# Reordered split, modulation and gate work in a hybrid decoder layer, with the last FFN block kept on the core

## The chip, the core and the metric

The kernel runs on one core of a Trainium2 chip. A core has TensorE (PE, matmuls into PSUM), VectorE (DVE), ScalarE (ACT), GpSimd (POOL) and SyncE (SP), which here issues the DMA transfers; each engine takes its own instructions in its own order and waits on semaphores for the others. The metric is the device time of one execution in microseconds (us), the median over runs.

## The reference

One decoder layer on a sequence of 1024 tokens with 1024 channels, all in float32:

```python
mod = silu(c) @ w_ada + b_ada                      # adaLN: six vectors of 1024
shift1, scale1, gate1, shift2, scale2, gate2 = split(mod, 6)
h = rmsnorm(x, norm1_w) * (1 + scale1) + shift1
qa, ka, va, iq, ik, iw, qr, kr, vr, gr, ga, gb = split(h @ w_in)      # 7240 columns
# attention: 8 heads of 64; a light indexer scores all keys, each query keeps its 256 best
y_a = sparse_attention(rope(qa), rope(ka), va, top256(indexer(iq, ik, iw))) @ w_attn_proj
# retention: 4 heads, keys of 128, values of 256, chunks of 128 tokens with a decayed state
y_r = (silu(gr) * head_groupnorm(retention(rot(qr), rot(kr), vr), gn_w)) @ w_ret_proj
x = x + gate1 * ((sigmoid(ga) * y_a + sigmoid(gb) * y_r) @ w_out)
h2 = rmsnorm(x, norm2_w) * (1 + scale2) + shift2
x = x + gate2 * ((silu(h2 @ w_ffn_gate) * (h2 @ w_ffn_up)) @ w_ffn_down)   # 2816 wide
return rmsnorm(x, final_norm_w)
```

## The kernel before

**Precision.** Each float32 matmul is done as three matmuls of rounded parts. A factor is split into a high part (a copy to a rounded type, ScalarE) and a low part (source minus high part, VectorE or GpSimd), and the product is high x high + high x low + low x high. A split is thus two instructions on two engines. In the names of tiles the endings `hi` and `lo` are these parts. `split_weight` (L70) splits projection weights, `split_block` (L760) the factors of the blocked products.

**Seven products instead of eight.** The gate, q and k projections, the FFN's two up products and the down product are multiplied by a Strassen-Winograd scheme: a 2 x 2 split of both factors, seven products `M1` to `M7` of block sums. Per stream of 256 weight columns (`class Stream`, L765) `ORDER` is M1, M5, M6, M3, M7, M2, M4; the token side's sums lie split in the tiles h11, S1, S2, S4, S3, h21, h22 (`SIDE`, L755). M1, M6, M7 and M4 accumulate in one PSUM bank, which is copied after M1 and M6 and added after M7; M5 and M3 share another. One product is 12 matmuls of 128 x 512. `run` (L873) emits the products of a sequence in order, prepares (loads, sums, splits) each factor two or three products ahead, and calls `behind(i)` after each product to place other work.

**Stages in order.** adaLN for the first norm; normed input `hT`; indexer; V of the attention with the indexer scores; retention, two heads at a time (`hp` = 0, 1), first Q and K for eight token tiles (rotation on GpSimd, transposes on TensorE), then V with the chunk work (`inner`, `chunk`); the gate streams (`flow`: four for gr, two for qa, two for ka, one for gb, four for ga); the retention projection; attention; merge; output projection with the second norm (`put_half1`, `put_half2`, `put_rest` split the normed tiles into the sides `h11`, `S1`, `h22`, `h21`); the FFN's 22 streams (`FfnEnv`), whose activations (`act_d`) and weight sums (`dw_d`) go through memory; the down product, which reads them back (`draw`) and splits them (`dslot`); final norm.

**Side work on VectorE.** The rest of adaLN (`mod_work`, L508) is a generator of 36 steps: four vectors of eight products of a 128 x 1024 weight tile (`mw`, two buffers, 512 KB a load on SP's queue) and one step that finishes the vector. Before, 16 steps lie beside the attention's V, 8 beside Q, K of heads 0 and 1, 9 beside their V, the rest after it. The selection of the 256 best (`select_all`, L449) is 32 counting passes of six instructions, a strict chain on VectorE. It has a low priority and fills holes; `passes` holds each pass's first instruction, and `turns_after(a, b)` only orders a after b on their engine, without a semaphore.

**What sets the order.** The kernel's text gives priorities, and a scheduler that simulates the engines' times lays out each engine's order from them; the orders given by `turns_after` bind it. So an edit at one place can move instructions elsewhere.

**Rotary part of q and k.** The qa and ka streams store their first 16 rows a head to `rot_d` and the rest to `q_d`, `k_d`. `rope_load` reads `rot_d` back, `rope_store` rotates it, splits it and stores it to `q_d` and `k_d` with eight DMAs a call.

## Time and profile before

| | |
|---|---|
| median of 3 runs | 1771.59 us (1771.57 to 1774.38) |
| the profiled execution | 1770.31 us, its span 1768.4 us |
| TensorE | busy 1696.3 us, 8266 matmuls, mean granted clock 0.991 |
| VectorE | busy 1216.7 us, 2099 instructions |
| ScalarE | busy 757.2 us, 1469 instructions |
| GpSimd | busy 882.4 us, 873 instructions |
| DMA | 266.48 MB, mean 151 GB/s |

"Busy" is the time in which an engine executes. A row of the waits names the engine, its line and tile, and what it waited for. A timeline row gives the start, the duration, the engine, the kernel's line, the operation with output and inputs, and in brackets the idle time before it and what ended it. PEld is TensorE's load of weights, which overlaps its matmuls.

### The profile page before, as it was taken

How to read it: one execution, taken by the hardware profiler on the slowest of the kernel's cores; microseconds unless marked ns; L12 is line 12 of the kernel's file. 1: busy time of each engine (PE TensorE's matmuls, PEld its weight loads, DVE VectorE, ACT ScalarE, POOL GpSimd, SP SyncE). 2: the span in 40 equal slices, each digit the busy share in tenths (PEclk: the TensorE clock that was granted, in tenths of full speed). 3: DMA queues.
4: the chain of work that ended last, by engine and by line, in shares of the span. 5: the costliest groups of instructions: out<-in, count | busy, mean ns of one | idle time of the engine just before them, and what ended most of it. 6: DMA issues, size and time to landing. Idle time of an engine off the chain costs nothing. (4 is left out here: it accounts for less than half of the span.)

```text
span 1768.4 us, 24625 instructions
## 1 busy us (share of the span) xinstructions
PE 1696.3 (96%) x8266; PEld 1393.6 (79%) x8266; DVE 1216.7 (69%) x2099; ACT 757.2 (43%) x1469; POOL 882.4 (50%) x873
## 2 busy tenths in 40 slices
PE   5899989999999999999999999899999999999998
PEld 4797768888878887788777888688787778787887
DVE  7529793888998687574675747865756565686665
ACT  3625533333544444430676146533333333444444
POOL 3563275683544678430355631054544445556564
PEclk9999999999999999999999999999999999999999
DMA  9535452512333355964843720134444444597762
GB/s 276 161 99 169 149 162 62 149 39 57 117 90 131 112 172 176 291 182 146 196 116 136 244 98 1 54 107 165 158 156 160 137 150 143 203 320 247 209 183 107
DMA packets 182654, 266.48 MB, mean 151 GB/s; under 512 B 13872, under 2 KB 111616, under 8 KB 180096
## 3 DMA queue, kind: packets, MB, share of 16 engines
q1 hardware_dynamic: 182528, 264.91, 48.1%
q8 instruction: 65, 1.06, 0.3%
q14 instruction: 61, 0.50, 0.1%
HBM read 195.39 MB, written 69.47 MB: 150 GB/s over the span
## 5 line engine op out<-in xcount | busy, mean ns | idle before, releaser
L80 POOL TENSOR_TENSOR wlo<-wraw,whi 128x512 fp32r<-128x512 f32 (+2 forms) x116 | 147.0, 1279 | 105.3 <-ACT whi L77 86.3
L463 DVE TENSOR_SCALAR_CACHE_REDUCE eq<-score,cand 128x384 uint8<-128x384 f32 (+2 forms) x192 | 180.5, 940 | 3.6
L762 POOL TENSOR_TENSOR flo<-tmp,fhi 128x512 fp32r<-128x512 f32 x79 | 107.1, 1356 | 139.7 <-ACT fhi L761 111.8
L121 PE MATMUL mm<-whi,hT_hi 128*128 128x512 f32 (+1 forms) x432 | 159.8, 376 | 3.8 <-ACT qk L650 1.8
L124 PE MATMUL mm<-whi,hT_lo 128*128 128x512 f32 (+1 forms) x432 | 161.5, 376 | 0.0
L123 PE MATMUL mm<-wlo,hT_hi 128*128 128x512 f32 (+1 forms) x432 | 160.3, 374 | 0.0
L838 PE MATMUL ya<-hc,fhi 128*128 128x512 f32 x344 | 134.6, 392 | 2.3 <-DVE c L821 1.4
L1604 DVE TENSOR_TENSOR dslot<-draw,dslot 128x512 fp32r<-128x512 f32 x88 | 94.7, 1107 | 58.4 <-ACT dslot L1603 54.2
L1603 ACT ACTIVATE dslot<-draw 128x512 fp32r<-128x512 f32 x154 | 90.4, 626 | 102.9 <-DMA draw<-dw_d 23.4
L840 PE MATMUL ya<-hc,fhi 128*128 128x512 f32 x344 | 133.9, 389 | 0.0
L842 PE MATMUL ya<-hc,flo 128*128 128x512 f32 x344 | 132.4, 389 | 0.0
L1604 POOL TENSOR_TENSOR dslot<-draw,dslot 128x512 fp32r<-128x512 f32 x66 | 98.0, 1498 | 65.4 <-ACT dslot L1603 61.7
L762 POOL TENSOR_TENSOR flo<-raws,fhi 128x512 fp32r<-128x512 f32 x60 | 82.1, 1369 | 92.7 <-ACT fhi L761 64.2
L77 ACT ACTIVATE whi<-wraw 128x512 fp32r<-128x512 f32 (+2 forms) x116 | 67.0, 590 | 112.0 <-DMA wraw<-in_w_in_dram 46.4
L840 PE MATMUL yb<-hc,fhi 128*128 128x512 f32 x256 | 100.6, 393 | 6.1 <-DVE hc L1295 6.1
L842 PE MATMUL yb<-hc,flo 128*128 128x512 f32 x256 | 100.7, 394 | 3.2 <-POOL flo L762 3.2
L761 ACT ACTIVATE fhi<-tmp 128x512 fp32r<-128x512 f32 x84 | 53.0, 631 | 113.1 <-PE ya L840 61.4
L838 PE MATMUL yb<-hc,fhi 128*128 128x512 f32 x256 | 100.6, 394 | 0.6 <-DVE c L821 0.4
L121 PEld LDWEIGHTS mm<-whi,hT_hi 128*128 128x128 f32 x432 | 80.9, 188 | 16.0 <-ACT qk L650 2.2
L1144 POOL TENSOR_SCALAR sx<-sx,mx 128x128 f32<-128x128 f32 (+7 forms) x64 | 47.8, 752 | 88.0 <-DVE mx L1143 65.1
L124 PEld LDWEIGHTS mm<-whi,hT_lo 128*128 128x128 f32 x432 | 81.3, 189 | 12.7 <-issue 0.5
L807 DVE TENSOR_TENSOR tmp<-raws 128x512 f32<-128x512 f32 x40 | 39.5, 989 | 74.3 <-POOL flo L762 74.3
(410 smaller groups left out, 4950.9 us busy)
## 6 DMA issues: line engine op xcount, KB each, us to landing
draw<-act_d SPq DMA_DIRECT2D x77, 256.0 KB
mw<-in_w_ada_dram SPq DMA_DIRECT2D x32, 512.0 KB
act_d<-c SPq DMA_DIRECT2D x64, 256.0 KB
raw<-in_w_in_dram SPq DMA_DIRECT2D x26, 512.0 KB
raws<-in_w_ffn_gate_dram SPq DMA_DIRECT2D x24, 512.0 KB
raws<-in_w_ffn_up_dram SPq DMA_DIRECT2D x24, 512.0 KB
dw<-in_w_ffn_down_dram SPq DMA_DIRECT2D x22, 512.0 KB
dw_d<-dw SPq DMA_DIRECT2D x11, 1024.0 KB
```

The lines of the kernel that those rows point to most:

```text
L77: ins = nc.scalar.activation(hi[:, :n], raw[:, :n], AF.Copy)
L80: nc.gpsimd.tensor_sub(lo[:, :n], raw[:, :n], f32(hi[:, :n]))
L121: ins = nc.tensor.matmul(ps, lhsT=ahi, rhs=whi[:, :n], start=(i == 0), stop=False)
L123: nc.tensor.matmul(ps, lhsT=ahi, rhs=wlo[:, :n], start=False, stop=False)
L124: nc.tensor.matmul(ps, lhsT=alo, rhs=whi[:, :n], start=False, stop=(i == last))
L463: ins = [nc.vector.tensor_scalar(eq[:, :sc.shape[1]], sc, thr[j], None, op0=op, op1=ALU.add, accum_out=cnt[:, j:j + 1]) for j, sc in enume ...
L762: (eng or nc.gpsimd).tensor_sub(lo, src, f32(hi))
L838: mm = nc.tensor.matmul(ps, lhsT=whi[:, k, :], rhs=hhi[:, k, :], start=own and k == 0, stop=False, skip_group_check=True)
L840: nc.tensor.matmul(ps, lhsT=whi[:, k, :], rhs=hlo[:, k, :], start=False, stop=False, skip_group_check=True)
L842: nc.tensor.matmul(ps, lhsT=wlo[:, k, :], rhs=hhi[:, k, :], start=False, stop=k == 3, skip_group_check=True)
L1603: nc.scalar.activation(slot[:, 0], raw, AF.Copy)
L1604: lo_eng.tensor_sub(slot[:, 1], raw, f32(slot[:, 0]))
```

## The change

- **adaLN:** no step of `mod_work` lies beside Q, K of heads 0 and 1 any more; two steps a tile, instead of one, lie beside their V. The passes get other places to stay behind: numbers 7 to 10 in V of heads 0, 1 and 18 to 21 in V of heads 2, 3 (before 1 to 3 in Q, K, 4 to 7 and 16 to 19), and from number 24 every seven products in the gate streams (before from 22 every six).
- **Gate streams:** the first two run M1, M5, M6, M2, M3, M7, M4; their low parts stay on VectorE five products longer; the last two streams' low parts go to VectorE instead of GpSimd. Both `rope_load` calls come at the stream of gb and both `rope_store` calls at the first ga stream; before, the second of each came one stream later.
- **Start of the FFN:** the last normed tile's `h11` and `h21` splits, the first factors and S2 come in a fixed order ahead of the later sums and splits (`in_turn`); the first two streams compute t1 early and in place; M6 stands ahead of M4; S4 and S3 are split three products later.
- **FFN streams:** M4 of a stream comes behind M1 of the next.
- **Last block of the FFN (p = 10):** its activations and weight sums aren't stored and loaded again; the down product splits them where they lie. The final norm's weights lie in two tiles instead of one, the squares in one scratch tile.

```diff
-    mod_ins = [None]
...
                 turns_after(ins, behind)
-            mod_ins[0] = ins
             yield
...
             nc.scalar.activation(qkT[t // 2][:, t % 2].rearrange("p h t -> p (h t)"), tp, AF.Copy)
-            if hp == 0:
-                next(mgen, None)
-                if t in (2, 4, 6):
-                    turns_after(passes[t // 2], mod_ins[0])
         slots = [rows_slot([(w_in, C_VR + 2 * DV * hp, 2 * DV)], k) for k in range(KT)]
...
             if t and t % 2 == 0:
-                turns_after(passes[(3, 15)[hp] + t // 2], chunked[0])
+                turns_after(passes[(6, 17)[hp] + t // 2], chunked[0])
             if hp == 0:
-                next(mgen, None)
+                for _ in range(2):
+                    next(mgen, None)
             elif t == 2:
...
         ins = nc.scalar.activation(hi, src, AF.Copy)
-        (eng or nc.gpsimd).tensor_sub(lo, src, f32(hi))
-        return ins
+        return ins, (eng or nc.gpsimd).tensor_sub(lo, src, f32(hi))
...
             self.early = ()
-            self.next = None
+            self.next = self.t1 = None
...
+        def sum_early(self):
+            b = self.blocks
+            self.t1 = b["12"]
+            nc.vector.tensor_sub(self.t1, b["12"], b["11"])
...
             elif m == "M4":
-                src = self.t2
-                nc.vector.tensor_sub(src, b["21"], src)
+                src = b["21"] if m in self.early else self.t2
+                self.env.in_turn(None, nc.vector.tensor_sub(src, b["21"], self.t2))
+            elif m == "M7" and "M4" in self.early:
+                src = four(self.env.tmp())
+                self.env.in_turn(None, nc.vector.tensor_sub(src, self.t2, b["11"]))
             else:
                 x, y = {"M5": ("12", "11"), "M6": ("22", None), "M7": ("22", "12")}[m]
-                if m == "M6" and "M5" in self.early:
+                if m == "M6" and "M5" in self.early and not self.t1:
                     self.t1 = src
-                    nc.vector.tensor_sub(src, b["12"], b["11"])
-                nc.vector.tensor_sub(src, b[x], b[y] if y else self.t1)
+                    self.env.in_turn(None, nc.vector.tensor_sub(src, b["12"], b["11"]))
+                self.env.in_turn(None, nc.vector.tensor_sub(src, b[x], b[y] if y else self.t1))
                 if m == "M5":
             hi, lo = self.env.slot()
-            self.split = split_block(src, hi, lo, self.env.lo_engine)
+            self.split, self.lo = split_block(src, hi, lo, self.env.lo_engine)
+            self.env.in_turn(self.split, self.lo)
             return hi, lo
...
+        def in_turn(self, *_):
+            pass
...
...
-    seq = [(st, m) for m in ORDER for st in flow[:2]]
+    seq = [(st, m) for m in ("M1", "M5", "M6", "M2", "M3", "M7", "M4") for st in flow[:2]]
     seq += [(st, m) for st in flow[2:-2] for m in ORDER]
...
         n, m = 2 + (i - 14) // 7, seq[i][1]
-        if i == 6:
-            genv.lo_engine = None
-        if i >= 15 and (i - 15) % 6 == 0 and 22 + (i - 15) // 6 < len(passes) - 1:
-            turns_after(passes[22 + (i - 15) // 6], genv.added)
+        if i in (11, n_mid - 4):
+            genv.lo_engine = None if i == 11 else nc.vector
+        if i >= 15 and (i - 15) % 7 == 0 and 24 + (i - 15) // 7 < len(passes) - 1:
+            turns_after(passes[24 + (i - 15) // 7], genv.added)
         if 14 <= i < n_mid:
                 flow[n].next = flow[n + 1]
-            if n in (8, 9) and m == "M1":
-                rope[n - 8] = rope_load(n - 8)
-            if n in (9, 10) and m == "M5":
-                rope_store(n - 9, *rope[n - 9])
+            if n == 8 and m in ("M1", "M7"):
+                rope[len(rope)] = rope_load(len(rope))
+            if n == 9 and m in ("M5", "M2"):
+                rope_store(int(m == "M2"), *rope[int(m == "M2")])
         if i == n_mid:
...
         hi, lo = (c[:, :, o:o + P] for c in combo[name])
-        nc.scalar.activation(hi, src, AF.Copy)
-        nc.vector.tensor_sub(lo, src, f32(hi))
+        ins = nc.scalar.activation(hi, src, AF.Copy)
+        return ins, nc.vector.tensor_sub(lo, src, f32(hi))
...
         h11, h21, h12, s1 = parts_of(o)
-        put_combo("h11", o, h11)
-        nc.vector.tensor_sub(s1, s1, h11)
+        ins = put_combo("h11", o, h11)
+        turns_after(nc.vector.tensor_sub(s1, s1, h11), ins[1])
+        return ins
         h11, h21, h12, s2 = parts_of(o)
-        put_combo("h21", o, h21)
+        ins = put_combo("h21", o, h21)
         nc.vector.tensor_sub(h21, h21, s2)
+        return ins
...
                         nc.vector.tensor_scalar(h_to, h_of, sc, sh, op0=ALU.mult, op1=ALU.add)
-            (put_half2 if th else put_half1)(o)
+            last_h11 = (put_half2 if th else put_half1)(o)
     alloc_combo("h21")
     for i in range(4):
-        put_rest(i * P)
+        last_h21 = put_rest(i * P)
     st_f.close()
...
         lo_engine = nc.vector
+        behind = []
+        def in_turn(self, scalar, vector):
+            for hi, lo in self.behind:
+                if scalar is not None:
+                    turns_after(scalar, hi)
+                turns_after(vector, lo)
...
     todo = []
+    last_act = {}
...
                      ("M3", s4)):
-            todo.append(lambda m=m, t=t: act_store(p, m, t))
+            if p < NP - 1:
+                todo.append(lambda m=m, t=t: act_store(p, m, t))
+            else:
+                last_act[m] = t
         if p:
...
         step(b21, b21, b22)
-        todo.insert(4, lambda: nc.sync.dma_start(out=dw_d[p], in_=dws[p]))
+        if p < NP - 1:
+            todo.insert(4, lambda: nc.sync.dma_start(out=dw_d[p], in_=dws[p]))
             hi, lo = (c[:, k, :] for c in combo[name])
-            nc.scalar.activation(hi, srcs[:, k, :], AF.Copy)
-            nc.vector.tensor_sub(lo, srcs[:, k, :], f32(hi))
+            ins = nc.scalar.activation(hi, srcs[:, k, :], AF.Copy), nc.vector.tensor_sub(lo, srcs[:, k, :], f32(hi))
+            fenv.in_turn(*ins)
+        return ins
...
         st.prepare("M1")
+        st.sum_early()
         turns_after(scaled[3], st.split)
+        turns_after(last_h11[1], st.lo)
+    fenv.behind = [last_h11, last_h21]
     s3 = ffn.tile([P, 4, H], F32, name="s3", tag="dw")
-    for st, after in zip(flow, (None, {0: 2}, {2: 3}, {0: 3})):
+    for st, after in zip(flow, (None, {0: 2}, {2: 3}, {1: 3})):
         st.product("M5", after)
             turns_after(scaled[3], st.copied)
-    split_combo("S2", hraw[1][:, 1])
-    seq = [(st, m) for m in ("M1", "M2", "M4", "M6", "M3", "M7") for st in flow[:2]]
+        else:
+            turns_after(st.copied, last_h11[0])
+    last_s2 = split_combo("S2", hraw[1][:, 1])
+    seq = [(st, m) for m in ("M1", "M2", "M6", "M4", "M3", "M7") for st in flow[:2]]
     n_first = len(seq)
+    for i in [i for i, (st, m) in enumerate(seq[:-1]) if m == "M4" and i >= n_first]:
+        seq[i:i + 2] = seq[i + 1], seq[i]
         st, m = seq[i]
-        if i == 0:
+        if i == 1:
+            fenv.behind += [(f.split, f.lo) for f in flow[:2]] + [last_s2]
+        if i == 4:
+            fenv.behind += [(f.split, f.lo) for f in flow[:2]]
             for k in range(4):
-                nc.vector.tensor_sub(s3[:, k, :], hraw[0][:, 0, k, :], hraw[1][:, 0, k, :])
-        if i == 1:
+                fenv.in_turn(None, nc.vector.tensor_sub(s3[:, k, :], hraw[0][:, 0, k, :], hraw[1][:, 0, k, :]))
             split_combo("S4", hraw[0][:, 1])
-        if i == 3:
+        if i == 6:
             split_combo("S3", s3)
             fenv.lo_engine = nc.gpsimd
+            fenv.behind = []
         if i == 9:
...
     n_slot = [0]
-    fnorm = ffn.tile([P, 4, H], F32, name="fnorm", tag="dw")[:, 0:2, :].rearrange("p a n -> p (a n)")
-    nc.sync.dma_start(out=fnorm, in_=final_norm_w.rearrange("(o d) -> o d", o=1).partition_broadcast(P))
-    nc.gpsimd.tensor_scalar(fnorm, fnorm, float(D ** 0.5), 1.0, op0=ALU.mult, op1=ALU.mult)
+    fnorm = [quad_tile("fnorm") for _ in range(2)]
+    for hf, fn in enumerate(fnorm):
+        nc.sync.dma_start(out=fn, in_=final_norm_w[hf * H:(hf + 1) * H].rearrange("(o d) -> o d", o=1)
+                          .partition_broadcast(P))
+        nc.gpsimd.tensor_scalar(fn, fn, float(D ** 0.5), 1.0, op0=ALU.mult, op1=ALU.mult)
     xo_all = slab_tile(7, [P, 8, H], F32, "xo")
-    def down_slot(src, lo_eng, scale=None):
+    def down_slot(src, lo_eng, scale=None, here=False):
         n_slot[0] += 1
-        raw, slot = raw_ring[:, n % 8, :], slot_rings[n // 4 % 6][:, n % 4]
-        nc.sync.dma_start(out=raw, in_=src)
+        raw, slot = src if here else raw_ring[:, n % 8, :], slot_rings[n // 4 % 6][:, n % 4]
+        if not here:
+            nc.sync.dma_start(out=raw, in_=src)
         if scale is not None:
...
     def down_factors(m, p):
-        s = down_slot(act_d[p][:, ACT_AT[m], :], nc.vector)
+        here = p == NP - 1
+        s = down_slot(last_act[m] if here else act_d[p][:, ACT_AT[m], :], nc.vector, here=here)
         if m in DW_AT:
+            if here:
+                return s, down_slot(dws[p][:, DW_AT[m], :], nc.gpsimd, here=True)
             src = dw_d[p][:, DW_AT[m], :]
...
-    ss3 = {}
+    ss3, squares = {}, []
             ss3[t] = const.tile([P, 16], F32, name="ss3", bufs=4)
-        sq = ffn.tile([P, H], BF16, name="sqh", tag="quad", bufs=10)
+        if not squares:
+            squares.append(ffn.tile([P, H], BF16, name="sqh", tag="quad", bufs=10))
+        sq = squares[0]
         nc.scalar.activation(sq[:, :c1 - c0], x1[t][:, c0:c1], AF.Square, accum_out=ss3[t][:, i:i + 1])
...
         nc.sync.dma_start(out=out[t * P:(t + 1) * P, H:], in_=xo[1])
-        nc.vector.scalar_tensor_tensor(xo[0], x1[t][:, :H], rs, fnorm[:, :H], op0=ALU.mult, op1=ALU.mult)
+        nc.vector.scalar_tensor_tensor(xo[0], x1[t][:, :H], rs, fnorm[0], op0=ALU.mult, op1=ALU.mult)
         nc.sync.dma_start(out=out[t * P:(t + 1) * P, :H], in_=xo[0])
         square(t, 0, H, 2 * H)
-        nc.gpsimd.tensor_mul(xo_all[:, (2 * t + 1) % 8, :], x1[t][:, H:], fnorm[:, H:])
+        nc.gpsimd.tensor_mul(xo_all[:, (2 * t + 1) % 8, :], x1[t][:, H:], fnorm[1])
     for m in ("M1", "M5", "M6", "M3", "M7", "M4"):
```

## The prediction

> **What bounds the kernel now.** I read the page's busy row first, then the waits of TensorE, then its timeline at each wait.

> ```profile
> PE 1696.3 (96%) x8266; PEld 1393.6 (79%) x8266; DVE 1216.7 (69%) x2099; ACT 757.2 (43%) x1469; POOL 882.4 (50%) x873
> ```

> TensorE is the path: 1696.3 of 1768.4 us busy, 72.1 us idle. The change removes and adds no matmul, so it can win only idle TensorE time and badly clocked TensorE time. The waits of TensorE (engine, tile, line waited for: us in total, times, longest) say where the idle time is; of the list I quote what the edits can reach.

> ```profile
> PE yb L840 <- DVE hc L1295: 6.1, 1, 6.1
> PE mm L838 <- ACT hT_hi L638: 3.5, 1, 3.5
> PE tr L666 <- POOL rq L663: 3.3, 2, 1.7
> PE yb L842 <- POOL flo L762: 3.2, 4, 0.8
> PE yb L1621 <- ACT dslot L1603: 3.0, 1, 3.0
> PE mm L838 <- DVE sums L821: 1.9, 1, 1.9
> PE ya L838 <- DVE c L821: 1.4, 4, 0.4
> PE lg L838 <- ACT kept L818: 1.2, 1, 1.2
> PE tr L667 <- POOL kk L663: 1.1, 1, 1.1
> PE ya L838 <- ACT c L818: 0.9, 4, 0.2
> PE mm L840 <- DVE hT_lo L639: 0.7, 1, 0.7
> ```

> Together 26.3 us. Behind four of the waits stands a second price. The stretches that begin at the end of the waits of 3.5, 1.9, 6.1 and 3.0 us, and one undisturbed stretch (stretch: length, busy, matmuls, granted clock, DMA):

> ```profile
> 517.61:521.30 3.69, 3.69 (x10) 0.56 0.51 142
> 712.41:716.06 3.65, 3.65 (x11) 0.53 0.65 165
> 1125.22:1129.13 3.91, 3.91 (x10) 0.52 0.00 0
> 1607.46:1613.81 6.35, 6.35 (x15) 0.51 0.61 192
> 1614.27:1620.62 6.35, 6.35 (x30) 1.00 0.65 201
> ```

> The last is 0.21 us a matmul. The four did 10, 11, 10 and 15 at about half clock, so they lost 3.69 - 10 x 0.21 = 1.6, 1.3, 1.8 and 3.2 us, 7.9 in all. Such time looks busy and goes when its wait goes. The reachable sum is 26.3 + 7.9 = 34.2 us.

> [...]

> **The change part by part.**

> *adaLN out of Q, K of the retention.* The stage's rotation runs on GpSimd, and TensorE waits for it (timeline rows: start, us, engine, line):

> ```profile
> 257.62 1.52 DVE L529 SCALAR_TENSOR_TENSOR macc<-mw,colT,macc 128x1024 f32<-128x1024 f32 x1
> 258.14 2.15 POOL L657 TENSOR_TENSOR rra<-qk,cosr 128x512 f32<-128x512 f32 x1
> 264.41 1.30 POOL L657 TENSOR_TENSOR rra<-qk,cosr 128x512 f32<-128x512 f32 x1
> 265.06 1.01 DVE L463 TENSOR_SCALAR_CACHE_REDUCE eq<-score,cand 128x768 uint8<-128x768 f32 x1
> 263.97 0.33 PE L666 MATMUL tr<-ident,rq 128*128 128x128 f32 x1 [1.69 <-POOL rq L663]
> ```

> Beside an adaLN product the rotation takes 2.15 us, beside a count of the selection 1.30. With eight products moved out, the three waits (3.3 + 1.1 = 4.4 us) go: the counts that fill VectorE instead don't lengthen GpSimd. I take 4.4; ends 2 and 4.4.

> *What that adds to V.* Eighteen generator steps instead of nine lie beside V of heads 0, 1.

> ```profile
> 285.00:350.00 65.00, 65.00 (x317) 55.10 (x316) 43.56 (x107) 21.63 (x45) 31.40 (x55) 1.00 0.40 116
> GB/s 276 161 99 169 149 162 62 149 39 57 117 90 131 112 172 176 291 182 146 196 116 136 244 98 1 54 107 165 158 156 160 137 150 143 203 320 247 209 183 107
> DMA packets 182654, 266.48 MB, mean 151 GB/s; under 512 B 13872, under 2 KB 111616, under 8 KB 180096
> 329.42 2.44 DVE L529 SCALAR_TENSOR_TENSOR macc<-mw,colT,macc 128x1024 f32<-128x1024 f32 x1 [0.59 <-DMA mw<-in_w_ada_dram]
> ```

> VectorE (third busy figure) has 65.0 - 43.6 = 21.4 us free there; eight to ten more products of 1.2 us need about 12. They also bring some nine loads of 512 KB on SP's queue, ahead of the stage's `ret_d` stores and the next Q, K weights: 7.5 MB (116 GB/s x 65 us) become some 12, or 190 GB/s, less than many slices of the page moved (second row). But a product that waits for its load, as the last row did for 0.59 us, holds back the `inn` product and the state update queued behind it, and SP can't issue the weights queued behind a load that waits for a buffer. Cost 0 to 15 us; 1.5 taken, nearer the row (TensorE idled nowhere here at nine steps). The counts are only pushed along: their number on VectorE stays, with fewer beside the gate streams.

> *M2 third in the first gate streams, their low parts longer on VectorE.* S3's splits come too late for M7:

> ```profile
> 489.00:529.00 40.00, 35.77 (x149) 28.49 (x147) 40.00 (x58) 17.77 (x30) 20.75 (x11) 0.96 0.30 84
> 508.15 1.77 DVE L625 TENSOR_TENSOR sums<-sums,hT_hi 128x512 f32<-128x512 f32 x1
> 516.21 0.68 DVE L625 TENSOR_TENSOR sums<-sums,hT_lo 128x512 f32<-128x512 f32 x1
> 528.15 0.85 DVE L639 TENSOR_TENSOR hT_lo<-sums,hT_hi 128x512 fp32r<-128x512 f32 x1
> ```

> VectorE (third busy figure) had no free time in these 40 us; beside GpSimd's low parts a step costs 1.77 instead of 0.68. Two M2 products put 2 x 12 x 0.21 = 5.1 us ahead of M3 and M7. Five low parts more on VectorE cost 5 x 0.6 = 3.0 us, and some eight lengthenings of 1.1 us go, so S3 ends about 5 us earlier too. Before, though, TensorE had already pulled other products into that hole, so not all of 3.5 + 0.7 + 1.6 = 5.8 us is sure. I take 4.0; ends 0 and 5.8.

> *Rotated q, k one stream back, last gate streams' low parts on VectorE.*

> ```profile
> 693.86 0.59 SPq L995 DMA_DIRECT2D q_d<-whi  x1
> 700.61 0.39 SPq L782 DMA_DIRECT2D raw<-in_w_in_dram  x1
> 705.87 0.63 ACT L761 ACTIVATE whi<-raw 128x512 fp32r<-128x512 f32 x1 [5.51 <-DMA raw<-in_w_in_dram]
> 709.21 1.75 DVE L807 TENSOR_TENSOR wraw<-raw,wraw 128x512 f32<-128x512 f32 x1 [6.16 <-POOL wlo L762]
> ```

> The last stream's weights stood on SP's queue behind the eight `q_d`, `k_d` stores; the load came at 700.61, ScalarE waited 5.51 us for it, GpSimd took five low parts in a row, VectorE waited 6.16 us for those and TensorE 1.9 us for VectorE. Three products (7.6 us) earlier, the stores are off that queue in time. I take 1.9 + 1.3 = 3.2; ends 0 and 3.2. The wait of 1.2 us on `kept` comes from the first store, which stays where it is: 0 taken, end 1.2. The second store could make the same wait at its new place: down to -1.2.

> *Splits of the last normed tile first.* At the start of the FFN:

> ```profile
> 1110.63 1.14 ACT L761 ACTIVATE fhi<-raws 128x512 fp32r<-128x512 f32 x2
> 1116.64 1.17 ACT L1294 ACTIVATE hc<-hraw 128x512 fp32r<-128x512 f32 x2
> 1124.48 1.28 DVE L1295 TENSOR_TENSOR hc<-hraw,hc 128x512 fp32r<-128x512 f32 x2
> ```

> The high halves of h11 and h21 stood by 1117.8, but VectorE took factor differences and S3's differences first and the low halves only at 1124.48; M1 waited 6.1 us. The new order puts the low halves first and the rest behind them; M1's own low parts must precede them, and can, since its high parts end at 1111.8 (first row). So 6.1 + 1.8 = 7.9 us go. What is late next: VectorE did S2, S3, S4 partly under that wait. M2 (5 us after M1) needs 0.6 + 1.2 us of VectorE; M6 needs nine steps of 0.6 by 1128, M4 four, S4 with M3 seven, S3 with M7 twelve and about eight additions by 1145, all within the time but with only some us to spare. I take 7.0; ends 3 and 7.9. M6 ahead of M4 and the early t1 are in this count.

> *M4 behind the next stream's M1.* Waits of 0.9 (M6 for the copy of M1) and 1.4 us (M4 for M7's addition) get one product (2.5 us) more and go; the four waits of 0.8 us for GpSimd's low part I leave. I take 2.3; ends -4 (new waits of 0.2 us at nineteen seams) and 5.5.

> *Last block's factors kept on the core.* This removes 7 `act_d` stores, one `dw_d` store of 1 MB and 11 `draw` loads from SP's queue:

> ```profile
> 1589.75 3.83 DVE L1502 TENSOR_TENSOR dw<-dw 128x512 f32<-128x512 f32 x4
> 1593.61 0.32 SPq L1513 DMA_DIRECT2D dw_d<-dw  x1
> 1606.78 2.71 ACT L1603 ACTIVATE dslot<-draw 128x512 fp32r<-128x512 f32 x5 [3.15 <-DMA draw<-dw_d]
> ```

> The weight sums end at 1593.6, their way through memory at 1606.8. Kept, ScalarE splits them 13 us earlier, and 3.0 + 3.2 = 6.2 us go; ends 5 and 6.2. `fnorm` becomes two loads and two GpSimd products, far ahead of use: 0.

> **The sum.** 4.4 - 1.5 + 4.0 + 3.2 + 0 + 7.0 + 2.3 + 6.2 = 25.6 us gained. The instruction order of all engines is laid out anew, so I take 1.5 us off for small waits at new places: 24.1. The profiled execution took 1770.3 us (span 1768.4 and 1.9 around it), 1.3 below the median of 1771.6; 1770.3 - 24.1 = 1746.2.

> **The rivals.**

> *S3 and the FFN's first streams stay late.* For it: VectorE was busy through both stretches, and work done under the old wait must now be done without it. Against: the contention with GpSimd leaves. The gate part gives 0 and the FFN start 3 us: 1746.2 + 4.0 + 4.0 = about 1754.

> *The adaLN loads hold up V.* If the 12 MB came at 151 GB/s, the page's mean, they would take 80 us, 15 more than the stage: 1746.2 + 15 = about 1761. Against: the page's slices reach 320 GB/s. [...]

> *Slower: the seam.* M1 of the next stream takes a slot pair, a bank and its raw weights one product sooner, M4 holds its own longer, at nineteen seams. If each makes TensorE wait 2 us the loss is 38 us: 1770.3 - 21.8 + 38 = about 1786. It decides from (24.1 - 2.3) / 19 = 1.15 us a seam. Against: the longest wait in these streams is now 0.8 us.

> *Little happens.* Every removed wait is followed at once by the next late one, as each hole was filled by other work: about 1768. Against it are the separate causes at six places.

> **How the numbers follow.** Forecast 0.60 (own range 1739 to 1750); late S3 and FFN start 0.20; adaLN loads 0.08; seam 0.05; little 0.03; all ends reached, 1736 to 1739, 0.04. The range 1736 to 1759 holds the first, second and last. A measurement tells about 0.2% (3.5 us) from no change: faster 0.92, same 0.03, slower 0.05.

> **What would show it.** Right: no TensorE wait on L663, on the h11 low halves, or on the last `dslot`; clock 1.00 near 520, 1125 and 1600 of the old time; TensorE's idle near 48 us. Wrong: waits on `mw` between 280 and 350 followed by TensorE idle; S3 still named by a TensorE wait; new waits on `fhi` or `raws` at each seam.

## The result and the profile after

| | before | after |
|---|---|---|
| median | 1771.74 us (1771.57 to 1774.38, 4 runs) | 1744.57 us (1744.32 to 1744.79, 4 runs) |
| ratio | | 0.9843, 95% interval 0.9826 to 0.986 |
| span of the profiled execution | 1768.4 us | 1742.7 us |
| TensorE's mean granted clock | 0.991 | 0.995 |

The change gains 27 us; the forecast was 1746.2. From the page of the changed kernel, its busy row; then from its waits of TensorE the rows that answer to those shown of before.

```profile
PE 1685.4 (97%) x8266; PEld 1391.7 (80%) x8266; DVE 1234.4 (71%) x2118; ACT 755.3 (43%) x1469; POOL 856.8 (49%) x855
```

```profile
PE tr L674 <- DVE inn L676: 4.7, 2, 3.4
PE lg L841 <- ACT whi L755: 2.1, 1, 2.1
PE ya L841 <- DVE c L824: 2.0, 2, 1.7
PE mm L841 <- DVE kept L824: 2.0, 1, 2.0
PE lg L841 <- ACT kept L821: 1.4, 1, 1.4
PE ya L843 <- DVE hc L1302: 0.6, 1, 0.6
PE mm L843 <- DVE hT_lo L636: 0.3, 1, 0.3
```

TensorE's idle time fell from 72.1 to 57.3 us and its busy time from 1696.3 to 1685.4. The waits on the rotation (`rq`, `kk`), `hT_hi`, GpSimd's `flo` and the last `dslot` are gone, that on `hc` is 0.6 instead of 6.1 us, that on S3's low parts (`hT_lo`) 0.3 instead of 0.7. New are 4.7 us on `inn` (the masked product of k and q of one chunk) in the retention, 2.0 on `kept` (partial results of a stream) and 2.1 on `whi` (high parts of weights) in the gate streams, and 1.7 on `c` (the FFN streams' partial results) at 1529, ahead of the streams' last product. Stretches of the changed kernel (columns as before: length, busy times with counts of PE, PEld, DVE, ACT, POOL, granted clock, DMA):

```profile
290.85:294.10 3.25, 3.25 (x9) 2.70 (x10) 2.99 (x4) 0.38 (x1) 0.00 (x0) 0.50 0.62 182
508.00:528.00 20.00, 19.82 (x88) 16.09 (x86) 20.00 (x31) 9.71 (x16) 10.24 (x7) 1.00 0.24 71
1114.00:1134.00 20.00, 19.42 (x86) 15.73 (x86) 19.96 (x34) 14.50 (x27) 0.00 (x0) 1.00 0.17 53
1570.00:1590.00 20.00, 20.00 (x90) 16.57 (x89) 16.75 (x15) 11.43 (x21) 14.02 (x9) 1.00 0.60 185
```

In the first gate streams, at the start of the FFN and at its last block, three of the four places where the prediction showed half clock, the clock is full; the last section comes to the fourth. One stretch at half clock is new, at 291, behind the first wait on `inn`.

Where the time went is seen best by stages, each from the start of one matmul to that of another in the profiled execution (us):

| stage | before | after |
|---|---|---|
| to the last matmul of the indexer's scores | 231.5 | 229.9 |
| retention, to its last state update | 234.2 | 236.4 |
| to the first product of the gate streams | 24.1 | 24.4 |
| gate streams, to the first transpose of g | 235.0 | 231.2 |
| attention, merge, output projection, to the first M1 of the FFN | 393.2 | 392.0 |
| FFN streams, to their last product | 434.1 | 417.5 |
| down product | 209.4 | 203.9 |

The first row holds no edit; it was 228.8 to 232.9 in the 12 further executions, so one execution tells some 2 us in that stage. The FFN streams gave 16.6 of the 25.7 us. The retention became longer.

### The profile page after: what moved, and what is told of

The parts are those of the page before. It is cut to its first block, busy times and chain, and to the rows that moved or that the text cites. A ratio compares the mean times of both kernels' runs of the same rounds, so it can differ in the third digit from the quotient of the medians.

```text
span 1742.7 us, 24594 instructions
## 1 busy us (share of the span) xinstructions
PE 1685.4 (97%) x8266; PEld 1391.7 (80%) x8266; DVE 1234.4 (71%) x2118; ACT 755.3 (43%) x1469; POOL 856.8 (49%) x855
## 4 chain that ended last, share of the span: by engine, by line
PE 64%; DVE 3%; issue 1%; DMA 1%; POOL 1%; ACT 1%; SPq 0%; POOLq 0%; DVEq 0%; ACTq 0%
PE ya L843 4%; PE ya L841 4%; PE ya L845 4%; PE yb L843 3%; PE yb L841 3%; PE yb L845 3%; PE ya L1664 2%; PE ya L1663 2%; PE ya L1662 2%; PE pva L1183 2%; PE mm L841 2%; PE mm L843 2%; PE mm L845 2%; PE tra L1162 2%; PE lg L841 1%; PE lg L843 1%
## 5 line engine op out<-in xcount | busy, mean ns | idle before, releaser
L463 DVE TENSOR_SCALAR_CACHE_REDUCE eq<-score,cand 128x384 uint8<-128x384 f32 (+2 forms) x192 | 180.7, 941 | 4.0
L1641 ACT ACTIVATE dslot<-draw 128x512 fp32r<-128x512 f32 x143 | 84.9, 627 | 93.1 <-DMA draw<-act_d 23.2
L756 POOL TENSOR_TENSOR flo<-raws,fhi 128x512 fp32r<-128x512 f32 x60 | 86.3, 1445 | 73.8 <-ACT fhi L755 42.4
L1642 DVE TENSOR_TENSOR dslot<-draw,dslot 128x512 fp32r<-128x512 f32 x81 | 86.4, 1098 | 50.7 <-ACT dslot L1641 49.3
L809 DVE TENSOR_TENSOR tmp<-raws 128x512 f32<-128x512 f32 x40 | 30.6, 768 | 86.7 <-POOL flo L756 86.7
```

Of the source, the lines that this page charges most:

```text
L463: ins = [nc.vector.tensor_scalar(eq[:, :sc.shape[1]], sc, thr[j], None, op0=op, op1=ALU.add, accum_out=cnt[:, j:j + 1]) for j, sc in enume ...
L756: return ins, (eng or nc.gpsimd).tensor_sub(lo, src, f32(hi))
L1641: nc.scalar.activation(slot[:, 0], raw, AF.Copy)
L1642: lo_eng.tensor_sub(slot[:, 1], raw, f32(slot[:, 0]))
```

## The experiments

Each kernel is the changed one with one edit. Times are medians over 4 to 6 runs. The kernel before, on the same chip, took 1769.49 us beside the kernels with adaLN, the seam, the last block and the fixed order undone, 1769.97 beside those with the product order of the FFN, the gate order and the rope undone and the first of the better versions, 1767.88 beside the unaltered kernel and the last two versions, and 1770.36 beside the one without rotation; the ratios are to these.

**adaLN and the passes put back.**

```diff
+            if hp == 0:
+                next(mgen, None)
+                if t in (2, 4, 6):
+                    turns_after(passes[t // 2], mod_ins[0])
...
-                turns_after(passes[(6, 17)[hp] + t // 2], chunked[0])
+                turns_after(passes[(3, 15)[hp] + t // 2], chunked[0])
...
-                for _ in range(2):
-                    next(mgen, None)
+                next(mgen, None)
...
-        if i >= 15 and (i - 15) % 7 == 0 and 24 + (i - 15) // 7 < len(passes) - 1:
-            turns_after(passes[24 + (i - 15) // 7], genv.added)
+        if i >= 15 and (i - 15) % 6 == 0 and 22 + (i - 15) // 6 < len(passes) - 1:
+            turns_after(passes[22 + (i - 15) // 6], genv.added)
```

> The changed kernel with its adaLN part alone undone: eight generator steps beside Q, K of heads 0 and 1 again, one a tile beside V, and the passes' old places. By the theory from the trace after (the doubled steps cost V a wait of 3.4 us with half clock behind it and one of 1.3 us, more than the 4.4 us won in Q, K): about 2.4 us faster than the changed kernel, 1742. By the prediction's own step (4.4 won, 1.5 lost): about 2.9 us slower, 1747.5. The Q, K waits on the rotation come back in both.

1745.31 us (1743.09 to 1747.49), 0.9868 (0.9853 to 0.9882). TensorE's timeline in Q, K of heads 0, 1:

```profile
252.60 0.33 PE L667 MATMUL tr<-ident,kk 128*128 128x128 f32 x1 [1.09 <-POOL kk L663]
258.57 0.33 PE L666 MATMUL tr<-ident,rq 128*128 128x128 f32 x1 [1.54 <-POOL rq L663]
264.99 0.33 PE L666 MATMUL tr<-ident,rq 128*128 128x128 f32 x1 [1.88 <-POOL rq L663]
```

The rotation's waits are back, 4.5 us, and yet the stage is 237.6 us, only 1.2 longer than after. The distance of matmul starts tells it better than the rows of waits. These stretches hold the stage's first 230 matmuls, mainly Q and K of heads 0 and 1, in the kernel before and in the changed one (counts are of matmuls that touch the stretch):

```profile
231.52:290.30 58.78, 52.59 (x231) 40.41 (x230) 42.48 (x71) 20.50 (x53) 53.37 (x64) 0.97 0.43 130
229.93:283.05 53.12, 51.34 (x232) 41.18 (x231) 51.13 (x96) 20.14 (x53) 47.30 (x64) 0.97 0.26 76
```

The change makes them 5.7 us shorter, and undone they take 60.4, with a stretch at half clock at 266 that the kernel before doesn't have. The rest of the stage takes 175.4 us before, 183.3 after and 177.1 undone. So the move takes 7.3 us out of Q, K and puts 6.2 into V. The wait on `kept` near 540 fell to 0.42 us, so that new wait belongs to the moved passes; but the gate streams take 231.7 us, no less than after, with waits of 1.6 us on the partial results (`spare`) and 2.8 on `kept` elsewhere.

**M4 ahead of the next stream's M1 again.**

```diff
-    for i in [i for i, (st, m) in enumerate(seq[:-1]) if m == "M4" and i >= n_first]:
-        seq[i:i + 2] = seq[i + 1], seq[i]
```

> The changed kernel with the FFN's products in the old order: M4 ahead of the next stream's M1. If a wait of TensorE costs what the starts of its matmuls show (0.3 to 0.4 us more than the idle time in its row), the seams are worth about 8 us: 1752.5. If it costs the idle time of its row (0.24 + 0.35 + 0.80 in four sets, of which some stays): 1748 to 1750. By the prediction's term of 2.3 us: 1747.

1756.0 us (1750.02 to 1761.01), 0.9928 (0.9908 to 0.9948). Its waits in the streams, then 390 us of the streams of the changed kernel and of this one, then two rows of TensorE's timeline of this one:

```profile
PE yb L845 <- POOL flo L756: 3.2, 4, 0.8
PE ya L841 <- DVE c L824: 1.4, 4, 0.4
PE ya L841 <- ACT c L821: 0.9, 4, 0.2
```

```profile
1140.00:1530.00 390.00, 387.98 (x1711) 320.90 (x1710) 248.92 (x273) 145.81 (x253) 204.37 (x145) 1.00 0.46 155
```

```profile
1146.00:1536.00 390.00, 383.86 (x1673) 312.38 (x1673) 239.63 (x265) 143.51 (x247) 191.68 (x141) 1.00 0.45 151
```

```profile
1289.26 0.39 PE L843 MATMUL yb<-hc,fhi 128*128 128x512 f32 x1
1290.44 0.50 PE L845 MATMUL yb<-hc,flo 128*128 128x512 f32 x1 [0.80 <-POOL flo L756]
```

The FFN streams take 426.8 us, 9.4 more, and the down product 1.1 more. All three kinds of wait of before return, GpSimd's low parts among them. By the rows of idle time the cost is small: 6.14 against 2.02 us idle in 390. But in the same 390 us at full clock 38 matmuls fewer start, and at 390 / 1711 = 0.228 us each that is 8.7 us. The last two rows show why: the wait is listed as 0.80, while the starts are 1.18 apart instead of 0.23, 0.95 lost, and the next start is late too, 0.34 behind (1290.78).

**The last block through memory again.**

```diff
-            if p < NP - 1:
-                todo.append(lambda m=m, t=t: act_store(p, m, t))
-            else:
-                last_act[m] = t
+            todo.append(lambda m=m, t=t: act_store(p, m, t))
...
-        here = p == NP - 1
+        here = False
```

(and `dw_d` is stored for every block).

> The changed kernel with the last FFN block's activations and weight sums stored and loaded again. The wait of 3.0 us before the down product's second pass and 3.2 us of half clock come back: about 6.2 to 6.6 us slower, 1751. Rival: the new order of the seams has moved the weight sums early enough, and the way through memory is hidden: 1745.

1750.36 us (1746.86 to 1756.52), 0.9902 (0.9882 to 0.9921). TensorE's timeline, and the stretch behind that wait:

```profile
1593.69 1.00 PE L1658 MATMUL yb<-dslot 128*128 128x512 f32 x2 [2.52 <-ACT dslot L1637]
```

```profile
1593.69:1596.50 2.81, 2.81 (x7) 2.24 (x8) 1.63 (x2) 1.80 (x4) 2.81 (x3) 0.55 0.81 248
```

The wait and its half-clocked stretch return: 2.5 us, and 7 matmuls in 2.81 us (1.2 lost). The down product takes 208.7 instead of 203.9 us, 4.8, of which these two are 3.7. The rest of the difference in span is the retention, below.

**No fixed order behind the h11 and h21 splits**, but M6 ahead of M4, the early t1 and the later S4, S3 kept.

```diff
-        turns_after(last_h11[1], st.lo)
-    fenv.behind = [last_h11, last_h21]
...
-            turns_after(st.copied, last_h11[0])
+            pass
```

> The changed kernel without the fixed order behind the last normed tile's h11 and h21 splits; M6 ahead of M4, the early t1 and the later S4 and S3 stay. If the order of the low halves was the cause of the wait of 6.1 us and the 1.8 us of half clock, most of 7.9 us comes back: about 1752. If it was enough that S3 and S4 come three products later and t1 earlier, less than 2 us: 1745 to 1746.5.

1743.83 us (1740.95 to 1751.21), 0.9868 (0.9847 to 0.9888). And the other half of that part undone, **M4 ahead of M6, S3's differences, S4 and S3 at their old places**, the fixed order kept:

```diff
-    seq = [(st, m) for m in ("M1", "M2", "M6", "M4", "M3", "M7") for st in flow[:2]]
+    seq = [(st, m) for m in ("M1", "M2", "M4", "M6", "M3", "M7") for st in flow[:2]]
...
-        if i == 4:
+        if i == 0:              # S3's differences; S4 at i == 1, S3 at i == 3
```

> M4 ahead of M6 again in the first two FFN streams, S3's differences, S4's and S3's splits at their old places; the fixed order behind the h11 and h21 splits and the early sum stay. Theory of the prediction: the low halves first are what takes the wait of 6.1 us away, so it stays away: M1 and M2 go on time, at most some waits under 1 us, 1744.5-1746. Rival, from the kernel without that fixed order (0.9 us of wait only, time unchanged): the later S3, S4 and the new order of M6 and M4 did it; then a wait of 2 us or more returns in the first FFN streams, for S2, M4's or M6's factors, 1747-1751.

1746.92 us (1745.04 to 1751.52), 0.9877 (0.9855 to 0.99). TensorE's timeline at the start of the FFN, of the first of the two kernels and of the second; then VectorE's of the changed kernel:

```profile
1113.13 0.73 PE L841 MATMUL yb<-hc,fhi 128*128 128x512 f32 x2 [0.73 <-ACT hc L1301]
```

```profile
1134.17 0.50 PE L845 MATMUL ya<-hc,flo 128*128 128x512 f32 x1 [1.15 <-DVE flo L756]
```

```profile
1112.66 1.28 DVE L756 TENSOR_TENSOR flo<-raws,fhi 128x512 fp32r<-128x512 f32 x2
1113.86 1.28 DVE L1302 TENSOR_TENSOR hc<-hraw,hc 128x512 fp32r<-128x512 f32 x2
```

Neither half brings the 6.1 us back. Without the fixed order the way from the output projection's last product to M1 takes 0.9 us more (14.1 for 13.2), with the old product order the streams take 1.3 more (418.8 for 417.5). Each half alone does nearly all, beside the early t1, which both kernels keep: low halves first is then enough, and so is taking the sums for S3 and the factors of M4 out of their way. What the early t1 does by itself, and whether the wait returns with both halves undone, no run shows.

**The first gate streams in the old order.**

```diff
-    seq = [(st, m) for m in ("M1", "M5", "M6", "M2", "M3", "M7", "M4") for st in flow[:2]]
+    seq = [(st, m) for m in ORDER for st in flow[:2]]
...
-        if i in (11, n_mid - 4):
-            genv.lo_engine = None if i == 11 else nc.vector
+        if i in (6, n_mid - 4):
+            genv.lo_engine = None if i == 6 else nc.vector
```

> The first two gate streams in the old order (M2 next to last) and GpSimd's low parts from the seventh product on, all else as changed. Theory: the order hid S3's splits; the waits of 3.5 and 0.7 us for S3's high and low parts return with a half-clock window (1.6 us lost): gate streams to the first g transpose 231.2 to about 235, time 1747-1749. Rival: it was the moved adaLN and counts that let S3 end earlier, or the hole was filled with other products: below 1 us of difference, 1744-1745.5.

1757.06 us (1747.64 to 1758.52), 0.992 (0.9894 to 0.9946). TensorE's timeline:

```profile
525.99 0.50 PE L841 MATMUL mm<-hT_hi,whi 128*128 128x512 f32 x1 [2.94 <-ACT hT_hi L635]
532.89 0.50 PE L843 MATMUL mm<-hT_lo,whi 128*128 128x512 f32 x1 [2.30 <-DVE hT_lo L636]
```

Both waits for S3 return and the stage takes 234.7 us, against 229.9 to 231.7 in the nine executions of the changed kernel and of its one-edit versions so far that have M2 third: 3 to 5 us for this part, so the theory held and the rival (the moved adaLN did it) falls. The order and the longer low parts on VectorE were undone together; how they share the gain is open. The time itself rose by more than the stage, and more than the 1747 to 1749 expected; the rest is again the retention, 244.2 us.

**Rotated q, k at the old places.**

```diff
-            if n == 8 and m in ("M1", "M7"):
-                rope[len(rope)] = rope_load(len(rope))
-            if n == 9 and m in ("M5", "M2"):
-                rope_store(int(m == "M2"), *rope[int(m == "M2")])
+            if n in (8, 9) and m == "M1":
+                rope[n - 8] = rope_load(n - 8)
+            if n in (9, 10) and m == "M5":
+                rope_store(n - 9, *rope[n - 9])
```

> Loads and stores of the rotated q, k where they were (load of the second half with the next stream's M1, its store at the M5 after that), all else as changed (low parts on VectorE in the last gate streams too). Theory of the prediction: 1.9 us of wait and 1.3 of clock return, 1747.8. Rival: the new place of the second store costs what it won, since ScalarE waits 1.7 us for the rotated sums with the next weights' splits behind it and TensorE 2.1 us for those; that wait goes, the old ones return in part because the last streams' low parts are now on VectorE: 1743.5-1745.5.

1745.33 us (1739.21 to 1752.34), 0.9862 (0.9835 to 0.9889). TensorE's longest wait at that place in this kernel, then what the changed kernel shows there (VectorE, ScalarE, TensorE):

```profile
711.78 0.50 PE L841 MATMUL mm<-hT_hi,whi 128*128 128x512 f32 x1 [1.02 <-DVE sums L824]
```

```profile
689.58 1.77 DVE L996 TENSOR_TENSOR wlo<-wlo,whi 128x512 f32<-128x512 f32 x1
691.38 0.63 ACT L755 ACTIVATE whi<-wlo 128x512 fp32r<-128x512 f32 x1 [1.73 <-DVE wlo L996]
694.14 0.50 PE L841 MATMUL lg<-hT_hi,whi 128*128 128x512 f32 x1 [2.12 <-ACT whi L755]
```

The gate streams take 230.0 us, none longer than after. At its new place the second store makes ScalarE wait 1.73 us for the rotated sums, with four splits of the next weights queued behind it, and TensorE 2.12 us for those. The old wait of 1.9 comes back as 1.0 only, in a kernel whose last low parts stay on VectorE. The move as such won nothing; what the low parts on VectorE give was not run by itself.

**What the retention's stage loses.** With the changed code of this stage it took 235.6 to 236.4 us in three executions and 241.9 to 244.3 in five, in kernels that differ only later. The difference is one instruction. The timelines of VectorE, of GpSimd and of TensorE of the unaltered changed kernel in a second execution, where the stage took 244.3 us (of GpSimd the first and the last of ten rows, 12 operations, without idle time between them):

```profile
391.84 8.76 DVE L468 TENSOR_SCALAR rej<-cnt 128x6 int32<-128x6 f32 x1
400.63 0.17 DVE L483 SCALAR_TENSOR_TENSOR cand<-cand,rej 128x6 int32<-128x6 int32 x1
...
418.03 0.29 DVE L676 TENSOR_TENSOR inn<-tr,rmask 128x128 f32<-128x128 f32 x1
```

```profile
389.98 2.54 POOL L80 TENSOR_TENSOR wlo<-wraw,whi 128x512 fp32r<-128x512 f32 x2
...
400.12 0.45 POOL L660 TENSOR_TENSOR kk<-rra,rrb 128x128 f32<-128x128 f32 x1
```

```profile
418.37 1.01 PE L674 MATMUL tr<-qkT 128*128 128x128 f32 x3 [7.65 <-DVE inn L676]
```

and the same step in the first execution, of 236.4 us:

```profile
393.33 0.70 DVE L468 TENSOR_SCALAR rej<-cnt 128x6 int32<-128x6 f32 x1
394.06 1.21 DVE L483 SCALAR_TENSOR_TENSOR cand<-cand,rej 128x6 int32<-128x6 int32 x1
```

A step on six elements a partition, 0.17 us elsewhere (at 408.26 in the first execution), is held for 8.76 us, until GpSimd's unbroken run of rotation and low parts ends at 400.57. The counts and the first `inn` of heads 2, 3 stand behind it, and TensorE waits 7.65 instead of 1.31 us. The same was seen with 8.77 to 8.80 us in four of the edited kernels, always to the end of such a run, and with 6.27 us in the kernel with adaLN put back, so the moved products are not needed for it. This is the kernel that was run unaltered beside the two best versions:

> The changed kernel, unaltered, beside the two that follow. Theory: in some executions the small step on 6 elements behind a count near 391 us is held up for 8.8 us by GpSimd, and inn near 417 then makes TensorE wait 7.7 instead of 1.3 us; so its times fall in two groups, about 1744 and about 1752, and the profile shows the retention's stage at 236 or 244 us. Rival: the two groups belong to the edited kernels alone; all its times lie within 1743 to 1746.

1744.34 us, 0.9865 (0.9848 to 0.9882); its four runs took 1741.47, 1743.25, 1745.42 and 1751.54, and the slowest, 6 us above the others, is the profiled execution with the step of 8.76 us. So the held step belongs to the changed kernel too; whether its times form two groups, four runs don't show. Beside the kernel before on this chip (1767.88) the gain is 23.5 us, where the first chip gave 27 with four executions within 0.5 us. To see whether GpSimd is the cause, the next leaves the rotation of heads 2, 3 out (q and k stay unrotated, ScalarE copies them):

```diff
+                if hp:
+                    nc.scalar.activation(dst, qk[:, hs], AF.Copy)
+                    continue
                 nc.gpsimd.tensor_sub(dst[:, :, 0, :], ra[:, hs, 0, :], rb[:, hs, 0, :])
```

> The changed kernel with the rotation of q, k of heads 2 and 3 left out (GpSimd's seven operations a tile; ScalarE copies q and k unrotated instead), so that in this stage GpSimd has only the weights' low parts and gaps between them. The laid-out order also puts the first inn one count sooner, so only the steps themselves are to be compared. Theory: the selection's two small steps a count are held up while GpSimd's operations follow one another without a gap; with gaps they can be held for one operation (1.3 us) at most, the 14 of the stage take 2.5 to 5 us together instead of 8.7 (15.0 in the execution with the 8.76 us step), and the runs no longer fall in two groups 8 us apart: all within 5 us, at 1736-1742. Rival: the steps are slow for a reason of their own (what they wait for, or the selection's chain); then the 14 take 8 us or more again and a step of over 3 us shows.

1739.35 us (1736.43 to 1741.81), 0.9823 (0.9809 to 0.9836). 51 us of that stage of the changed kernel and of this one, and this one's longest step:

```profile
362.00:413.00 51.00, 50.20 (x234) 41.15 (x232) 49.02 (x99) 17.80 (x43) 36.08 (x50) 1.00 0.18 45
```

```profile
362.00:413.00 51.00, 51.00 (x244) 42.27 (x243) 48.04 (x117) 20.21 (x52) 13.30 (x17) 1.00 0.18 47
```

```profile
394.88 1.25 DVE L468 TENSOR_SCALAR rej<-cnt 128x6 int32<-128x6 f32 x1
```

With GpSimd at 13.3 instead of 36.1 us the 14 small steps take 3.4 us together instead of 8.7 (15.0 in the other execution), and none over 1.25, about the time of one GpSimd operation (1.29 to 1.30 for the low parts there). The spread of the runs, 5.4 us, is just over what was expected, but no run stands apart. The theory held: GpSimd's run holds the step.

The other wait of the stage, 3.38 us at 291, is the one that the prediction named as a danger (VectorE, then TensorE, of the changed kernel):

```profile
289.31 1.28 DVE L527 SCALAR_TENSOR_TENSOR macc<-mw,colT,macc 128x1024 f32<-128x1024 f32 x1 [0.52 <-DMA mw<-in_w_ada_dram]
290.51 0.28 DVE L676 TENSOR_TENSOR inn<-tr,rmask 128x128 f32<-128x128 f32 x1
290.85 0.80 PE L674 MATMUL tr<-qkT 128*128 128x128 f32 x2 [3.38 <-DVE inn L676]
```

The first `inn` stands behind adaLN products that wait for their loads, 0.52 us here and 0.80 at 283.56.

**Versions without these waits.** No adaLN step beside the first V tile, and one pass fewer before the V of heads 2, 3:

```diff
-                turns_after(passes[(6, 17)[hp] + t // 2], chunked[0])
+                turns_after(passes[(6, 16)[hp] + t // 2], chunked[0])
...
-                for _ in range(2):
+                for _ in range(2 if t else 0):
...
-        if i >= 15 and (i - 15) % 7 == 0 and 24 + (i - 15) // 7 < len(passes) - 1:
-            turns_after(passes[24 + (i - 15) // 7], genv.added)
+        if i >= 15 and (i - 15) % 6 == 0 and 23 + (i - 15) // 6 < len(passes) - 1:
+            turns_after(passes[23 + (i - 15) // 6], genv.added)
```

> No adaLN step beside the first V tile of heads 0, 1, and one count of the selection fewer before the V of heads 2, 3 (it goes behind the gate streams, whose counts stand 6 instead of 7 products apart). Theory: what the moved adaLN costs is two waits of TensorE for inn, 3.4 us near 291 behind a product whose load is late and 1.3 us (7.7 in two other executions of the same code) near 413 behind the counts, of which the small step on 6 elements is held up for 0.7 to 8.8 us while GpSimd works without a gap. Both go, and a half-clock window with the first: the retention's stage falls from 236.4 to 229-231 us, the time to 1738-1741. Rival: VectorE has too much work in this stage, so the wait comes back at another inn or state update: 236 us and 1744-1746. Second rival: the count pushed into the first gate streams makes S3 late: stage shorter, but TensorE waits 2 us or more for S3's splits or kept near 530, in all 1742-1744.

1742.9 us (1740.62 to 1744.12), 0.9847 (0.9825 to 0.987): a miss in size. The stage fell to 235.5 us only:

```profile
285.75 0.49 PE L674 MATMUL tr<-qkT 128*128 128x128 f32 x2 [0.77 <-DVE inn L676]
411.23 0.49 PE L674 MATMUL tr<-qkT 128*128 128x128 f32 x2 [2.44 <-DVE inn L676]
```

The first wait went from 3.38 to 0.77, but two steps were held for 5.02 and 3.37 us and the second `inn` was late again. So the next takes out one pass more (`(6, 15)`, 22 and six), and parts `rope_store` in two: the sums at M1 and M3, the splits and stores at M6 and M2 of the same stream.

> No adaLN step beside the first V tile; two counts fewer before the V of heads 2, 3 (they go to the gate streams, 6 products apart); the sums of the rotated q, k two products ahead of their splits, so that ScalarE does not wait for them with weight splits queued behind. Theory: an inn is no longer behind the counts even when a small step is held up for 8.8 us, and the waits of 2.1 and 1.4 us at the q, k stores go: retention 232-234 us, gate streams 228-230, time 1735-1739, and no second group. Rival: VectorE is full from the V of heads 2, 3 to the first gate streams, so the two counts make S3 late and kept wait longer than 2.0 us: 1742-1745.

1738.76 us (1737.29 to 1744.34), 0.9845 (0.9824 to 0.9865). No wait on `inn` is left and the retention takes 230.9 us, although steps were held for 5.03 and 3.36 us; the gate streams take 230.5, with the wait on `kept` at 2.1 still there. The last one holds the pass that stands ahead of that addition:

```diff
+        if i == 13:
+            turns_after(passes[20], genv.added)
```

> As the kernel before it, and the count that stands ahead of the additions to kept in the first gate streams is held behind the last of them. Theory: the wait of 2.0 us for kept near 536 is VectorE's count ahead of the addition; it goes, 2 to 2.5 us less: 1733-1737. Rival: the addition is late because S3's low parts are; the wait stays, and the counts pushed together behind it delay later additions: same time or up to 2 us more.

1734.87 us (1733.5 to 1735.97), 0.9816 (0.9802 to 0.9831), beside 1744.34 (1741.47 to 1751.54) of the changed kernel on the same chip: 9.5 us less, no run of the one within the runs of the other. Of its waits in V and in the gate streams these are the longest:

```profile
PE lg L689 <- ACT on L698: 1.2, 1, 1.2
PE lg L841 <- ACT kept L821: 1.0, 1, 1.0
```

The retention takes 230.6 us and the gate streams 225.8.

## Why the prediction was right, step by step

The total (24.1 forecast, 25.7 in the spans) came out because errors of both signs cancelled: V and the rotated q, k fell some 9.6 us short of their terms, and the seams gave 8.2 more than theirs. That the sum came within 2 us is luck.

- **adaLN out of Q, K, 4.4:** the cause is right. The waits went, and 4.5 us of them came back when it was undone. By the starts it is 5.7 us, since the price was again taken from rows of waits.
- **V, 1.5 lost:** the step that failed. The retention should have become 2.9 us shorter and is 2.2 longer: 5.7 us won in Q, K, 7.9 lost behind it, and 15.8 in the execution with the held step, just past the end of 15. When the part was undone, 6.2 of the 7.9 came back; the other 1.7 stay open (one step was held for 6.27 us there too). The late load ahead of `inn` was the mechanism named, but the size was taken from a stage with half as many products. The hold was not seen: "the counts that fill VectorE instead don't lengthen GpSimd" is true (the rotation's product takes 1.29 to 1.30 us from 237.83 to 270.58), yet GpSimd holds the counts' small steps, for up to 8.76 us, and more of these stood ahead of an `inn`. As a whole the part won nothing that the runs show: 0.9868 of the time before with it undone, 0.9843 and 0.9865 for the changed kernel in its two measurements.
- **First gate streams, 4.0:** right (3 to 5 by the kernel with the old order). The new wait of 2.0 us on `kept` behind a pass was not in it.
- **Rotated q, k, 3.2:** wrong. The end that was priced and not taken (the second store makes the same wait at its new place) is what happened; undoing the move lost nothing.
- **Start of the FFN, 7.0:** the size is right, by 7.2 us (excess of the starts over 0.227 us a matmul, from the first M1 to 1140: 8.1 before and 0.9 after). Of the cause only half was named: beside the early t1 either of two halves of the edit is enough.
- **Seams, 2.3:** mis-sized; 9.4 us in the streams and 1.1 in the down product. Two reasons. The four waits for GpSimd's `flo` were left standing and went too, and each wait was priced by its row: 13 waits of 6.0 us in the rows cost 9.4 more than 2 of 2.0 us, 0.5 us a wait beyond its row.
- **Last block, 6.2:** 4.8 us when undone; the way through memory was the cause, a little below the end of 5.
- **Small waits, 1.5 off:** the new waits on `kept` and `whi` take 4.1 us.
- **Idle and clock:** idle TensorE time was to be near 48 us and is 57.3. The 48 is 72.1 less the whole gain of 24.1, a slip: up to 7.9 of that gain was clock, which the profile lists as busy time, so the prediction's own terms give some 56. Busy time fell by 10.9 us. Part of what a wait costs is listed as busy time, as the seam showed (9.4 us, against 4.0 in the rows).

Of the rivals, the adaLN loads holding up V came true in part; the seam went the other way. Two of the prediction's signs of being wrong showed: the wait on `mw` at 289, with 3.38 us of idle TensorE behind it, and S3 still named by a wait, of 0.3 us.

## What to carry to other kernels

Price a short wait of a matmul stream by the distance of the starts around it, not by its idle row (here 0.95 us and 0.34 behind it, against 0.80), and count all waits that an edit gives more time, not those of one cause. When work moves from one stage to the next on an engine, list what then stands ahead of the first product that the next stage needs: here the waits on `inn` took back what Q, K had won. A small instruction of VectorE was held here for 8.76 us by a long unbroken run on GpSimd, so what must be on time should not stand behind a chain of them.

## What the runs showed of the hardware that was not expected

**The hold by GpSimd.** One VectorE step of 0.17 us took 3.4 to 8.8 us in nine of the profiled executions: 8.76 from 391.84 in the changed kernel's second, through eleven GpSimd operations to the end of their unbroken run at 400.57, and 8.77 from 392.66 to 401.43 in the kernel with M4 back at its old place, where such a run ended at 401.40. In the changed kernel's first execution it got through after 0.70 us, in the moment between two operations (393.33 + 0.70, where the next GpSimd operation began at 393.96). Without the rotation the longest was 1.25. By what the one holds the other, no run shows.

**The starts of half clock lay multiples of 3.413 us apart.** A wait of 2.17 us on `whi` in the changed kernel's second execution was followed by half clock, the same wait of 2.12 us (694.14, above) in the first by full clock, and one of 2.94 us (525.99) in the kernel with the old gate order by full clock. Below are stretches of 3.41 us: with the wait of the second execution, which ended at 700.77, and behind it; around the wait in the first execution; and around that of the old gate order.

```profile
697.16:700.57 3.41, 1.44 (x7) 0.86 (x5) 3.34 (x7) 2.57 (x5) 2.11 (x3) 1.00 0.58 179
700.57:703.98 3.41, 3.21 (x8) 2.54 (x9) 3.37 (x6) 2.05 (x5) 3.41 (x3) 0.50 0.61 207
```

```profile
690.07:693.48 3.41, 1.95 (x9) 1.29 (x7) 3.34 (x6) 2.10 (x5) 2.12 (x3) 1.00 0.56 177
693.48:696.89 3.41, 2.75 (x12) 2.19 (x13) 3.37 (x6) 2.03 (x5) 3.41 (x3) 1.00 0.55 187
```

```profile
521.10:524.51 3.41, 1.94 (x9) 1.29 (x7) 3.41 (x3) 0.00 (x0) 3.41 (x3) 1.00 0.01 3
524.51:527.93 3.42, 1.95 (x8) 1.61 (x9) 3.42 (x7) 1.93 (x4) 0.80 (x2) 1.00 0.00 0
```
